# Splitting the first activation chunks and loading their weights further ahead, in a fused encoder block on one Trainium2 core

## The chip, the cores and the metric

One NeuronCore of a Trainium2 chip runs the whole program in one launch. Its engines work side by side, each in its own program order: PE (TensorE, matrix products), DVE (VectorE), ACT (ScalarE), POOL (GpSimd) and SP (SyncE, which here only issues DMAs). Semaphores make an instruction wait for data from another engine or from a DMA. The metric is the device time of one execution in microseconds; a change is judged by the median of several executions.

## The reference, cut to what matters

The block has 512 tokens of width 1024. First comes an adaLN-conditioned mixer (a gated convolution and a gated recurrence, one input and one output projection), then a PEER layer: every token looks up its best 16 of 16384 one-neuron experts in each of 8 heads and adds their outputs. The change lies in the PEER layer:

```python
def block(xb):                                   # in the reference over blocks of 128 tokens
    q = (xb @ w_q).reshape(p, PEER_HEADS, 2, PEER_DK_HALF)
    sc = jnp.einsum('phcd,hcnd->phcn', q, sub_keys)
    top_s, top_i = lax.top_k(sc, PEER_TOPK)      # 16 best of 128 keys, twice a head
    cand_s = (top_s[:, :, 0, :, None] + top_s[:, :, 1, None, :]).reshape(p, PEER_HEADS, kk)
    best_s, best_pos = lax.top_k(cand_s, PEER_TOPK)
    idx = jnp.take_along_axis(cand_i, best_pos, axis=-1)
    g = jax.nn.softmax(best_s, axis=-1)
    act = jax.nn.gelu(jnp.einsum('phkd,pd->phk', expert_u[idx], xb), approximate=False)
    return jnp.einsum('phk,phkd->pd', g * act, expert_v[idx])
```

## The kernel before

The kernel does the PEER layer in two ways at once. For 320 of the 512 tokens it is **dense**: all 16384 activations of a token are computed, multiplied by a gate matrix that is zero except at the token's 128 chosen experts, and multiplied by all of expert_v. For the other 192 tokens it is **sparse**: the chosen rows of expert_u and expert_v are gathered from HBM by POOL's indirect DMAs (L1044), and DVE makes dot products (L1065, in `dots`) and sums (L1082, in `sums`) of them. 64 of the sparse tokens (index tile `idx_b`) take only their dot products this way.

The dense half has 128 chunks of 128 experts. The first phase (L1277 to L1325, the loop over k below CE = 124) is the activation phase: step k makes the products of expert_u chunk k with the 320 tokens on PE (`u_chunk`), eight blocks of 128 in depth, and ACT applies Gelu into a tile (`u_evict`, L1149). The second phase (L1364 to L1394) multiplies the gated activations by the chunks of expert_v (`v_chunk`, L1348). Four expert_u chunks are left for the second phase.

Precision: a float32 operand is split into a high part in the faster fp32r format and a low part that holds the rest. `high` (L74) is an ACT copy, `low` (L79) a subtraction on DVE or on POOL; `mm3` (L88 to L90) makes three products a block: high by high, high by low, low by high. Chunks 1 to 11 (k below FN = 12) are different: they use the unsplit float32 weights and an unsplit copy of the tokens, `h2f`, with one matmul a block (L1158), and need neither high nor low. ACT writes `h2f` at L674, in the norm before the query projection.

Weights are loaded by SP, 512 KB a chunk, into a rotating pool `wraw` of WR = 4 tiles; chunks 5 to 11 use the pools `wlo` and `whi` in place of it. `w_ahead(k)`, called at the start of step k, issues loads up to chunk k + 4. High halves are made three steps ahead (`w_high(k + 3)`), low halves two steps ahead (`w_low(k + 2)`).

Activations of two chunks share a tile `act` of 2 x 320 columns, 16 of them (RB = 32 chunks). The first 48 pairs are written to HBM at step 2q + 4 (`spill`, to `Ad`) and read back in the second phase (`v_act`); the last ones stay in SBUF. Pairs 48 and up (v0 = 96) come first in the second phase.

The order of the activation phase is written out by a planner in the Python code (L1244 to L1315). It keeps counters of nanoseconds for PE, DVE and ACT (`pe`, `dve`, `ac`). Each step adds the costs of its chunk (L1166 to L1168) and then gives DVE pieces of other work until `dve` has caught up with `pe`: searches for the best keys (`topk_tile`, `stage1`), the gate matrix (`gates_tile`, with products of one-hot matrices on PE, L908) and dot products. A generator that yields a number has done work of that cost; one that yields None sleeps until the next step. What is not done by step KD = 118 is done there at once. The limit on dot products a step stands in `turn` (L1254): given["d"] counts them against DR = 1.25 a step, and `xd > k % 2` allows one in even steps and two in odd ones. The first gathers start when the search of token tile 1 has yielded its indices (`sready`).

The instructions from L670 to L1275 are ordered by the tile framework, which may move an instruction ahead of others on its engine; those of the loop stay in the order written.

Of the kernel before, what the change touches and what calls it, by code (L numbers as in the profile page):

```python
# [17 lines left out]
T = 512  # L18
# [16 lines left out]
def block_kernel(ctx, tc, xT, small, w_ada1, w_ada, b_ada, w_in, w_r, w_i, w_out, w_q, keys, uT, u, v, final_g, out):  # L35
# [618 lines left out]
    h2f = [ring.tile([128, 2, NU], F32, name="act", bufs=RB // 2) for _ in range(KB // 2)]  # L654
# [12 lines left out]
    for k in range(KB):  # L667
        if k == 2:
            qsp[1] = split_w(qraw[1])
            norm2.close()  # L670
        t1 = sq_pool.tile([128, T], F32, name="mt1")
        nc.vector.tensor_mul(t1, xs[:, k, :], psr2)
        modulate(t1, k, A2, adac[:, 24:32], h2h, h2l, full2)
        nc.scalar.activation(h2f[k // 2][:, k % 2], t1[:, T - NU:], AF.Identity, scale=A2[:, k:k + 1],  # L674
                             bias=adac[:, 24 + k:25 + k])
        if k < len(x1p):
            x1_out(*x1p[k])
# [61 lines left out]
    act0 = ring.tile([128, 2, NU], F32, name="act", bufs=RB // 2)  # L739
# [39 lines left out]
    def topk_tile(t):  # L779
# [30 lines left out]
        for w in range(2):  # L810
# [5 lines left out]
            if t == 1 and w == 0:  # L816
                yield None
# [281 lines left out]
    def w_load(k):  # L1099
        if k < len(jobs):  # L1100
            kind, i = jobs[k]
            if 5 <= k < FN:
                raw = wring.tile([128, KB, 128], FR, name=("wlo", "whi")[k % 2], bufs=WB).bitcast(F32)
                nc.sync.dma_start(raw, uT[i])
                wraw[k] = raw
                return
            if k >= K5 and (k - K5) % 5 == 4:
                wraw[k] = gp.tile([128, KB, 128], F32, name="raw5")
                nc.sync.dma_start(wraw[k], uT[i] if kind == "u" else
                                  v[vorder[i] * 128:(vorder[i] + 1) * 128, :].rearrange("p (k e) -> p k e", k=KB))  # L1110
                return
            wraw[k] = load_w(uT[i] if kind == "u" else
                             v[vorder[i] * 128:(vorder[i] + 1) * 128, :].rearrange("p (k e) -> p k e", k=KB))

    def w_high(k):
        if FN <= k < len(jobs):
            whi[k] = high(wraw[k])

    def w_low(k):
        if FN <= k < len(jobs):  # L1120
            wlo[k] = low(wraw.pop(k), whi[k])
            settle()
# [3 lines left out]
    def w_ahead(k):  # L1126
        while loaded[0] < k + (5 if k < K5 - 5 else 6):
            loaded[0] += 1
            w_load(loaded[0])
# [14 lines left out]
    def u_evict():  # L1144
        if unread:
            c, ps = unread.pop()
            if c % 2 == 0:
                act[c // 2] = ring.tile([128, 2, NU], F32, name="act", bufs=RB // 2)
            nc.scalar.activation(act[c // 2][:, c % 2], ps, AF.Gelu)  # L1149

    def u_chunk(k, pool):
        c = jobs[k][1]
        if c:
            ps = pool.tile([128, NU], F32, name="ps_act", bufs=3 if pool is psE else 2)
            if k < FN:
                raw = wraw.pop(k)
                for j in range(KB):
                    nc.tensor.matmul(ps, raw[:, j, :], h2f[j // 2][:, j % 2], start=j == 0, stop=j == KB - 1)  # L1158
            else:
                mm3(ps, whi.pop(k), wlo.pop(k), hd, ld, range(KB), True, True)  # L1160
# [5 lines left out]
        pe[0] += FPE if c and k < FN else 3530  # L1166
        dve[0] += 0 if c and k < FN - 2 else 1140
        ac[0] += 450 if c and k < FN - 3 else 1400  # L1168
# [41 lines left out]
    def v_act(q):  # L1210
        if q < NE // 2:
            c = vorder[2 * q] // 2
            if act[c] is None:
                act[c] = ring.tile([128, 2, NU], F32, name="act", bufs=RB // 2)
# [29 lines left out]
    pe, dve, ac = [0], [-HEAD], [0]  # L1244
# [6 lines left out]
    def turn(k):  # L1251

        awake = [g for g in "gsrd" if g in gens and asleep[g] <= k]
        if "d" in awake and (given["d"] >= DR * (k + 1 - first[0]) + DX * max(k - late_k.get("g", k), 0) or k >= CE - QU or xd > k % 2):  # L1254
            awake.remove("d")
# [21 lines left out]
    for k in range(CE):  # L1277
# [13 lines left out]
        dve[0] = max(dve[0], RHO * pe[0] - LEAD - (HEAD if k < 9 else 0))  # L1291
# [157 lines left out]
FN = 12  # L1449
DX = 0.3  # L1450
FPE = 4400
# [6 lines left out]
HEAD = 0  # L1458
# [9 lines left out]
RB = 32  # L1468
ZL = 1
# [54 lines left out]
```

## Time and profile before

| | us |
|---|---|
| median of 3 runs | 1323.59 |
| lowest and highest run | 1322.09, 1323.73 |
| the profiled execution | 1322.02 |
| its span | 1320.3 |
| PE, DVE, ACT, POOL busy in the span | 1302.8, 1210.0, 729.6, 508.7 |
| HBM read and written | 393.54 MB, 45.09 MB |

The span runs from the first to the last instruction; 1.7 us of the profiled execution lie around it. In time order: the mixer until about 207 us, norm and query projection until 279, the activation phase until about 773, the second phase until 1307, the last norm and the output until 1320. The page's line of DMA traffic, in 40 slices of 33 us:

```profile
GB/s 374 268 245 175 183 137 96 113 153 107 297 367 337 317 346 386 402 389 348 417 417 417 412 343 397 412 414 415 413 414 413 414 413 415 411 409 412 413 380 142
```

Slices 9 and 10 (280 to 330 us), the start of the activation phase, move little; from slice 19 on the rate is near 415 most of the time. Matmuls are pipelined, and the profile shows each with more time than passes between two of them, so the time of a chunk is read from the starts of successive chunks.

### The profile page before, as it was taken

Reading aid. Unit: us, or ns where it says so; the run is one execution under the profiler, and the core shown is the slowest. Engines: PE = TensorE matmul, PEld = TensorE weight load, DVE = VectorE, ACT = ScalarE, POOL = GpSimd, SP = SyncE. Lnnn points to the kernel's source line nnn. Section 1 sums busy time; section 2 is a strip of 40 time slices with the busy share of each in tenths; the row PEclk is TensorE's granted clock in tenths of the full one; section 3 lists DMA queues with packets and bytes.
Section 4 is the critical chain, followed back from the end, with each engine's and each line's share of the span. In section 5 each row is a group of like instructions: output and inputs, shape, how many; then the busy total and the mean of one; then the engine's idle time right before and its main releaser. Section 6 shows DMA issues by size and latency. Waiting matters only on the chain.

```text
span 1320.3 us, 21362 instructions
## 1 busy us (share of the span) xinstructions
PE 1302.8 (99%) x7506; PEld 1127.5 (85%) x7506; DVE 1210.0 (92%) x2241; ACT 729.6 (55%) x1319; POOL 508.7 (39%) x342
## 2 busy tenths in 40 slices
PE   8999999999999999999999999999999999999996
PEld 6677777777999999999999998888888888888885
DVE  6889975899999999999999679999899999899998
ACT  4677736424786987879669544333343434343433
POOL 0000002301133133434665537677555455565550
PEclk9999999999999999999999999999999999999999
DMA  9775542343899899999999999999999999999993
GB/s 374 268 245 175 183 137 96 113 153 107 297 367 337 317 346 386 402 389 348 417 417 417 412 343 397 412 414 415 413 414 413 414 413 415 411 409 412 413 380 142
DMA packets 151276, 440.06 MB, mean 333 GB/s; under 512 B 17024, under 2 KB 44672, under 8 KB 151168
## 3 DMA queue, kind: packets, MB, share of 16 engines
q1 hardware_dynamic: 104016, 267.23, 54.1%
q0 software_dynamic: 46864, 170.41, 32.7%
q8 instruction: 59, 0.97, 0.3%
q10 hardware_dynamic: 288, 1.05, 0.2%
q14 instruction: 49, 0.40, 0.1%
HBM read 393.54 MB, written 45.09 MB: 332 GB/s over the span
## 4 chain that ended last, share of the span: by engine, by line
PE 87%; issue 4%; DVE 3%; DMA 2%; POOL 2%; ACT 1%; DVEq 0%; SPq 0%; POOLq 0%; ACTq 0%
PE acc L1348 38%; PE ps_act L88 8%; PE ps_act L89 8%; PE ps_act L90 8%; PE ps_z L89 4%; PE ps_z L90 4%; PE ps_z L88 4%; PE ps_act L1158 4%; PE ps_gt L908 2%; POOL rows L1044 2%; PE ps_z L346 1%; DMA wraw<-in_uT_dram 1%; DMA rows<-in_u_dram,idx_s 1%; PE ps_g L732 1%; PE ps_row L138 1%
## 5 line engine op out<-in xcount | busy, mean ns | idle before, releaser
L74 ACT ACTIVATE whi<-wraw 128x1024 fp32r<-128x1024 f32 x255 | 269.7, 1058 | 235.6 <-DMA wraw<-in_v_dram 141.6
L79 DVE TENSOR_TENSOR wlo<-wraw,whi 128x1024 fp32r<-128x1024 f32 x249 | 303.2, 1218 | 34.4 <-ACT whi L74 33.7
L88 PE MATMUL ps_act<-h,whi 128*128 128x320 f32 x928 | 291.4, 314 | 0.0
L89 PE MATMUL ps_act<-h,whi 128*128 128x320 f32 x928 | 286.8, 309 | 0.0
L90 PE MATMUL ps_act<-h,wlo 128*128 128x320 f32 x928 | 286.7, 309 | 0.0
L1044 POOL DMA_INDIRECT rows<-in_u_dram,idx_s x128 | 207.5, 1621 | 142.5 <-DVE scr L1065 101.3
L1044 POOL DMA_INDIRECT rows<-in_v_dram,idx_s x128 | 192.1, 1501 | 158.3 <-DVE ys L1082 135.2
L1348 PE MATMUL acc<-wlo,ch 128*128 128x512 f32 x744 | 229.1, 389 | 0.0
L1348 PE MATMUL acc<-whi,ch 128*128 128x512 f32 x744 | 229.1, 389 | 0.0
L1348 PE MATMUL acc<-whi,cl 128*128 128x512 f32 x744 | 229.0, 389 | 0.0
L88 PEld LDWEIGHTS ps_act<-h,whi 128*128 128x128 f32 x928 | 174.2, 188 | 0.5
L89 PEld LDWEIGHTS ps_act<-h,whi 128*128 128x128 f32 x928 | 174.4, 188 | 0.2
L90 PEld LDWEIGHTS ps_act<-h,wlo 128*128 128x128 f32 x928 | 174.2, 188 | 0.0
L1044 POOL DMA_INDIRECT rows<-in_u_dram,idx_b x64 | 88.5, 1382 | 215.9 <-DVE scr L1065 152.9
L1082 DVE SCALAR_TENSOR_TENSOR ys<-rows,acts,ys 128x1024 f32<-128x1024 f32 x127 | 163.3, 1286 | 1.5
L1348 PEld LDWEIGHTS acc<-wlo,ch 128*128 128x128 f32 x744 | 139.7, 188 | 29.0
L1348 PEld LDWEIGHTS acc<-whi,cl 128*128 128x128 f32 x744 | 139.7, 188 | 29.0
L1348 PEld LDWEIGHTS acc<-whi,ch 128*128 128x128 f32 x744 | 139.5, 188 | 28.5
L1065 DVE SCALAR_TENSOR_TENSOR scr<-rows,h2n 128x1024 f16<-128x1024 f32 x128 | 156.1, 1220 | 6.7 <-DMA rows<-in_u_dram,idx_s 5.1
L1149 ACT ACTIVATE act<-ps_act 128x320 f32<-128x320 f32 x127 | 55.7, 439 | 112.7 <-PE ps_act L90 79.4
L896 ACT ACTIVATE igh<-oh,gl 128x128 f16<-128x128 f16 x320 | 99.5, 431 | 4.5 <-DVE oh L875 4.5
L1232 ACT ACTIVATE ch<-cf 128x768 fp32r<-128x768 f32 x64 | 54.2, 847 | 61.8 <-PE acc L1348 20.7
(326 smaller groups left out, 1884.1 us busy)
## 6 DMA issues: line engine op xcount, KB each, us to landing
wraw<-in_uT_dram SPq DMA_DIRECT2D x120, 512.0 KB, 7.6
wraw<-in_v_dram SPq DMA_DIRECT2D x103, 512.0 KB, 13.4
Gd<-stg SPq DMA_DIRECT2D x46, 512.0 KB, 9.1
wada<-in_w_ada_dram SPq DMA_DIRECT2D x45, 512.0 KB, 6.5
Ad<-act SPq DMA_DIRECT2D x48, 320.0 KB, 8.1
act<-Ad SPq DMA_DIRECT2D x48, 320.0 KB, 14.2
raw<-in_v_dram SPq DMA_DIRECT2D x25, 512.0 KB, 13.3
h<-Gd SPq DMA_DIRECT2D x48, 256.0 KB, 14.4
```

The lines of the kernel that those rows point to most:

```text
L74: nc.scalar.activation(hi, raw, AF.Copy)
L79: (eng or nc.vector).tensor_sub(lo, raw, hi.bitcast(F32))
L88: nc.tensor.matmul(ps, hi[:, k, :], xh(k), start=first and k == ks[0], stop=False)
L89: nc.tensor.matmul(ps, hi[:, k, :], xl(k), start=False, stop=False)
L90: nc.tensor.matmul(ps, lo[:, k, :], xh(k), start=False, stop=last and k == ks[-1])
L896: nc.scalar.activation(ig[:, 1, k // 2, :, k % 2], of[:, k // 2, 0, :, k % 2], AF.Copy, scale=gl[:, t0 + k:t0 + k + 1])
L1044: nc.gpsimd.indirect_dma_start(out=r[:, :], out_offset=None, in_=table, in_offset=bass.IndirectOffsetOnAxis(ap=idxs[:, k:k + 1], axis=0))
L1065: nc.vector.scalar_tensor_tensor(scr, rows.pop(n), 1.0, hn, op0=OP.mult, op1=OP.mult, accum_out=dst[:, k:k + 1])
L1082: nc.vector.scalar_tensor_tensor(ys, rows.pop(k), acts[:, k:k + 1], ys, op0=OP.mult, op1=OP.add)
L1149: nc.scalar.activation(act[c // 2][:, c % 2], ps, AF.Gelu)
L1232: nc.scalar.activation(ch, coef[q], AF.Copy)
L1348: nc.tensor.matmul(accs[b][e], st[:, bs], mv[:, e * 512:(e + 1) * 512], start=first, stop=last)
```

## The change

Chunks 1 to 11 go through `high`, `low` and `mm3` like the others; `h2f` and its eight ACT copies are gone. The low halves of chunks 1 to 9 (k below PL = 10) are made on POOL, the others on DVE. The 16 activation tiles become one tile `ringb`. Its first seven slots of 1024 columns (PB = 7) take weights as long as the activations kept there are not due (slot r until chunk v0 + 2 * (1024r // 640), that is 96, 98, 102, 104, 108, 112, 114); the spilled pairs use the last four activation slots in turn (SPS = 4). `w_ahead` issues up to two loads a step as slots come free, which gives up to 12 chunks ahead (7 slots and the 4 tiles of `wraw`), until k = 112. The planner's costs follow: 3530 for every chunk on PE, a low half on DVE is charged from step 8 on. The search of token tile 1 sleeps three more steps in all, and from step 92 on each step may take two dot products.

```diff
--- before.py
+++ after.py
@@ -651,7 +651,11 @@
     ring = ctx.enter_context(tc.tile_pool(name="ring", bufs=1, side="right"))
     ND = T - 128
     NU = ND - XB
-    h2f = [ring.tile([128, 2, NU], F32, name="act", bufs=RB // 2) for _ in range(KB // 2)]
+    ringb = ring.tile([128, RB * NU], F32, name="ringb")
+
+    def act_slot(i):
+        return ringb[:, 2 * NU * i:2 * NU * (i + 1)].rearrange("p (c t) -> p c t", c=2)
+
 
     def full2(k, f):
         if k % 4 == 0:
@@ -671,8 +675,6 @@
         t1 = sq_pool.tile([128, T], F32, name="mt1")
         nc.vector.tensor_mul(t1, xs[:, k, :], psr2)
         modulate(t1, k, A2, adac[:, 24:32], h2h, h2l, full2)
-        nc.scalar.activation(h2f[k // 2][:, k % 2], t1[:, T - NU:], AF.Identity, scale=A2[:, k:k + 1],
-                             bias=adac[:, 24 + k:25 + k])
         if k < len(x1p):
             x1_out(*x1p[k])
 
@@ -736,7 +738,7 @@
         for c in range(2):
             sc[h, c] = scs.tile([128, NT, 128], F32, name="sc", bufs=SCB)
             nc.scalar.activation(sc[h, c], pss[c], AF.Copy)
-    act0 = ring.tile([128, 2, NU], F32, name="act", bufs=RB // 2)
+    act0 = act_slot(RB // 2 - SPS)
     nc.scalar.activation(act0[:, 0], ps0, AF.Gelu)
     assert next(early, None) is None
     pro.close()
@@ -813,7 +815,8 @@
                 pf = topk.tile([128, 8, 16], F16, name="pf")
                 nc.vector.tensor_copy(pf, msk)
             yield None
-            if t == 1 and w == 0:
+            if t == 1:
+                yield None
                 yield None
             key, ref, cmp, src = ((pf, st16, OP.is_ge, dif), (pf, io16, OP.is_equal, tif[:, :, 1, :]))[w]
             nc.scalar.activation(oh, key[:, :, :, None].to_broadcast(shp), AF.Copy)
@@ -1096,37 +1099,51 @@
     v0 = max(CE - RB + 3, 0) // 8 * 8 + 8
     vorder = list(range(v0, NE)) + list(range(v0))
 
-    def w_load(k):
+    rfree, rold = [0] * PB, []
+
+    def w_load(k, at=0):
         if k < len(jobs):
             kind, i = jobs[k]
-            if 5 <= k < FN:
-                raw = wring.tile([128, KB, 128], FR, name=("wlo", "whi")[k % 2], bufs=WB).bitcast(F32)
-                nc.sync.dma_start(raw, uT[i])
-                wraw[k] = raw
-                return
             if k >= K5 and (k - K5) % 5 == 4:
                 wraw[k] = gp.tile([128, KB, 128], F32, name="raw5")
                 nc.sync.dma_start(wraw[k], uT[i] if kind == "u" else
                                   v[vorder[i] * 128:(vorder[i] + 1) * 128, :].rearrange("p (k e) -> p k e", k=KB))
                 return
+            for r in range(PB):
+                if 5 <= k <= v0 + 2 * (1024 * r // (2 * NU)) and rfree[r] <= at:
+                    rfree[r] = k - 1
+                    wraw[k] = ringb[:, 1024 * r:1024 * (r + 1)].rearrange("p (k e) -> p k e", k=KB)
+                    nc.sync.dma_start(wraw[k], uT[i])
+                    return
+            if k < K5 - 5:
+                assert len(rold) < WR or rold[-WR] <= at
+                rold.append(k - 1)
             wraw[k] = load_w(uT[i] if kind == "u" else
                              v[vorder[i] * 128:(vorder[i] + 1) * 128, :].rearrange("p (k e) -> p k e", k=KB))
 
     def w_high(k):
-        if FN <= k < len(jobs):
+        if k < len(jobs):
             whi[k] = high(wraw[k])
 
     def w_low(k):
-        if FN <= k < len(jobs):
-            wlo[k] = low(wraw.pop(k), whi[k])
+        if k < len(jobs):
+            wlo[k] = low(wraw.pop(k), whi[k], nc.gpsimd if k < PL else None)
             settle()
 
     loaded = [4]
 
     def w_ahead(k):
+        if k < K5 - 13:
+            for _ in range(2):
+                m = loaded[0] + 1
+                if any(f <= k and 5 <= m <= v0 + 2 * (1024 * r // (2 * NU)) for r, f in enumerate(rfree)) \
+                        or len(rold) < WR or rold[-WR] <= k:
+                    loaded[0] += 1
+                    w_load(m, k)
+            return
         while loaded[0] < k + (5 if k < K5 - 5 else 6):
             loaded[0] += 1
-            w_load(loaded[0])
+            w_load(loaded[0], k)
 
     def weights(k):
         w_ahead(k)
@@ -1145,27 +1162,23 @@
         if unread:
             c, ps = unread.pop()
             if c % 2 == 0:
-                act[c // 2] = ring.tile([128, 2, NU], F32, name="act", bufs=RB // 2)
+                q = c // 2
+                act[q] = act_slot(q - v0 // 2 if q >= v0 // 2 else RB // 2 - SPS + q % SPS)
             nc.scalar.activation(act[c // 2][:, c % 2], ps, AF.Gelu)
 
     def u_chunk(k, pool):
         c = jobs[k][1]
         if c:
             ps = pool.tile([128, NU], F32, name="ps_act", bufs=3 if pool is psE else 2)
-            if k < FN:
-                raw = wraw.pop(k)
-                for j in range(KB):
-                    nc.tensor.matmul(ps, raw[:, j, :], h2f[j // 2][:, j % 2], start=j == 0, stop=j == KB - 1)
-            else:
-                mm3(ps, whi.pop(k), wlo.pop(k), hd, ld, range(KB), True, True)
+            mm3(ps, whi.pop(k), wlo.pop(k), hd, ld, range(KB), True, True)
             u_evict()
             unread.append((c, ps))
         q = c // 2 - 2
         if c % 2 == 0 and 0 <= q < v0 // 2:
             spill(q)
-        pe[0] += FPE if c and k < FN else 3530
-        dve[0] += 0 if c and k < FN - 2 else 1140
-        ac[0] += 450 if c and k < FN - 3 else 1400
+        pe[0] += 3530
+        dve[0] += 0 if k < PL - 2 else 1140
+        ac[0] += 1400
 
     gbuf, g16, gdone = {}, {}, set()
     coef = {}
@@ -1211,7 +1224,7 @@
         if q < NE // 2:
             c = vorder[2 * q] // 2
             if act[c] is None:
-                act[c] = ring.tile([128, 2, NU], F32, name="act", bufs=RB // 2)
+                act[c] = act_slot(c % (RB // 2))
                 nc.sync.dma_start(act[c].rearrange("p c t -> p (c t)"), Ad[c])
 
     def v_gated(q):
@@ -1241,7 +1254,7 @@
 
     gens = {"s": searches_E(), "r": rest_E(), "g": gates_E(), "d": dots()}
     dot_gen = gens["d"]
-    pe, dve, ac = [0], [-HEAD], [0]
+    pe, dve, ac = [0], [0], [0]
     late_k = {}
     asleep = {"s": 0, "r": 0, "g": 0, "d": NE}
     given = {"s": 0, "r": 0, "g": 0, "d": 0}
@@ -1251,7 +1264,7 @@
     def turn(k):
 
         awake = [g for g in "gsrd" if g in gens and asleep[g] <= k]
-        if "d" in awake and (given["d"] >= DR * (k + 1 - first[0]) + DX * max(k - late_k.get("g", k), 0) or k >= CE - QU or xd > k % 2):
+        if "d" in awake and (given["d"] >= DR * (k + 1 - first[0]) + DX * max(k - late_k.get("g", k), 0) or k >= CE - QU or xd > (k % 2 if k < 92 else 1)):
             awake.remove("d")
         if gopen and "g" in gens:
             gt = 96 * (k + 1 - gopen[0]) / (KD - KG - gopen[0])
@@ -1288,7 +1301,7 @@
             for m in range(GB_E - 1):
                 gath(u, usteps[m][0], usteps[m][3], m)
         ac[0] = max(ac[0], pe[0] - LEAD)
-        dve[0] = max(dve[0], RHO * pe[0] - LEAD - (HEAD if k < 9 else 0))
+        dve[0] = max(dve[0], RHO * pe[0] - LEAD)
         xd = 0
         while dve[0] < RHO * pe[0] or k == KD:
             g = turn(k)
@@ -1446,16 +1459,14 @@
 GS = 32768.0
 AB = 3
 GPE = 460
-FN = 12
+PL = 10
 DX = 0.3
-FPE = 4400
 SE = 0.65
 AD = 500
 LEAD = 3500
 RHO = 1.0
 VE = 1
 KG = 4
-HEAD = 0
 NS = 56000
 DS = 1.0
 XD = 2
@@ -1466,6 +1477,8 @@
 QU = 6
 UV = 0.86
 RB = 32
+PB = 7
+SPS = 4
 ZL = 1
 XE = 5
 WB = 4
```

## The prediction

> **What bounds the kernel now.** I read the page first, for the engines' shares, then the table of stretches, to see whether one engine is the limit everywhere, then the timelines of TensorE (PE) and VectorE (DVE) chunk by chunk.
>
> ```profile
> span 1320.3 us, 21362 instructions
> ## 1 busy us (share of the span) xinstructions
> PE 1302.8 (99%) x7506; PEld 1127.5 (85%) x7506; DVE 1210.0 (92%) x2241; ACT 729.6 (55%) x1319; POOL 508.7 (39%) x342
> ```
>
> ```profile
> 212.90:228.80 15.90, 14.99 (x80) 9.49 (x78) 15.23 (x25) 15.49 (x24) 2.25 (x4) 1.00 0.37 129
> 280.00:327.00 47.00, 47.00 (x177) 33.23 (x176) 45.99 (x270) 14.18 (x20) 2.91 (x3) 1.00 0.35 119
> 327.00:420.00 93.00, 93.00 (x703) 92.27 (x702) 92.31 (x227) 66.13 (x140) 33.55 (x23) 1.00 0.94 326
> 420.00:526.00 106.00, 106.00 (x866) 104.16 (x866) 105.09 (x243) 92.68 (x212) 25.61 (x20) 1.00 0.96 352
> 640.00:735.00 95.00, 95.00 (x742) 93.68 (x741) 86.81 (x124) 74.31 (x195) 56.87 (x37) 1.00 1.03 417
> 735.00:770.00 35.00, 35.00 (x240) 35.00 (x240) 20.51 (x25) 14.07 (x22) 12.40 (x8) 1.00 1.04 390
> ```
>
> The columns are the stretch, its length, then PE, weight loads, DVE, ScalarE (ACT), GpSimd (POOL), the granted clock, the DMA share and GB/s. PE is busy in the whole activation phase (about 279 to 773 us), at full clock. DVE is close behind it up to 526 us (45.99 of 47, 92.31 of 93, 105.09 of 106) and has room only after 640 us. DMA runs at 417 GB/s from 640 to 735 us. So time is saved where PE has less to do or stops standing, as long as DVE keeps up. The same chain in the last phase:
>
> ```profile
> 803.16 489.62 PE acc L1348 x2160
> ```
>
> That is 227 ns for each of 2160 matmuls without a break, and the change adds nothing there: what the activation phase saves should reach the end.
>
> **The change, part by part. 1. Eleven chunks in three matmuls for one.**
>
> ```profile
> 296.57 4.47 PE L1158 MATMUL ps_act<-act,whi 128*128 128x320 f32 x16
> 300.88 4.47 PE L1158 MATMUL ps_act<-act,wlo 128*128 128x320 f32 x16
> ...
> 334.08 0.31 PE L88 MATMUL ps_act<-h,whi 128*128 128x320 f32 x1
> ...
> 337.60 0.31 PE L88 MATMUL ps_act<-h,whi 128*128 128x320 f32 x1
> ```
>
> One unsplit chunk takes 300.88 - 296.57 = 4.31 us, a split one (334.08 to 337.60, chunk 14) 3.52. Eleven chunks: 11 x 0.79 = **8.7 us less on PE**. [...]
>
> **2. The stand of PE at 632 us.**
>
> ```profile
> 631.18 1.06 ACT L74 ACTIVATE whi<-wraw 128x1024 fp32r<-128x1024 f32 x1 [2.97 <-DMA wraw<-in_uT_dram]
> ...
> 632.62 2.27 PE L908 MATMUL ps_gt<-igh,oh 128*128 128x128 f16 x15 [0.30 <-ACT igh L896]
> ...
> 641.98 0.93 PE ps_gt L908 x16
> ```
>
> ACT stood 2.97 us for a weight load, the gate products behind it on ACT (L896) came late, and PE, after 0.30 us idle, spent 2.27 us on 15 gate matmuls, 2.6 in all, where 16 usually take 0.93. It is the only place where chunk starts show such a stand. Loads issued up to 12 chunks ahead (they were 4) take that wait away: **1.7 us less**. Nothing else is late next there: DVE idles 8.2 us of that stretch.
>
> **3. Eight ACT copies into h2f go (L674).**
>
> ```profile
> L674 ACT ACTIVATE act<-mt,adac,A 128x320 f32<-128x320 f32 x8 | 5.1, 643 | 0.0
> ```
>
> 5.1 us of ACT, in a stretch (212.9 to 228.8) where ACT is busy 15.49 of 15.90 us. But DVE is busy 15.23 there, so no more than 0.7 can be had; bounds 0 and 0.7, I take **0.4 less**.
>
> **4. DVE's lead at the start.** The planner (L1244 to 1315) gives DVE work until its counter passes PE's. Walking through its counters for both versions gives the work of each step. Before, step 0 charged a low half (1140) that nobody made, and PE's first chunks were charged 4400 but took 4.31; both made a lead. After, lows 1 to 9 are charged nothing and chunks 3530 against a real 3.52.
>
> ```profile
> 281.36 0.27 DVE L690 MAX8 top<-sc 128x8 f32<-128x128 f32 x1
> ...
> 293.50 0.29 DVE L690 MAX8 top<-sc 128x8 f32<-128x128 f32 x1
> ...
> 322.62 1.22 DVE L79 TENSOR_TENSOR wlo<-wraw,whi 128x1024 fp32r<-128x1024 f32 x1
> 323.76 0.28 DVE L832 SCALAR_TENSOR_TENSOR best<-ij 128x128 f32<-128x128 f32 x1
> ...
> 335.46 1.20 DVE L79 TENSOR_TENSOR wlo<-wraw,whi 128x1024 fp32r<-128x1024 f32 x1
> ```
>
> The lead is thin already: chunk 15's low half ends at 336.66, and the chunk starts at 337.60. After: steps 0 to 2 have the same work as before, 281.36 to 293.50. Steps 3 to 6 have 11 half searches, 13.05 by the planner's costs, which the trace bears out for this kind; step 7 has 4.2 to 4.4. So the first low half on DVE (chunk 10) starts near 311.0 and ends near 312.1. PE would ask for it at 279.24 + 9 x 3.52 + 0.3 = 311.2. Seven low halves (1.14 each, 322.62 to 323.76) and 17.6 us of work later, chunk 17's ends near 337.8; PE would ask for it at 335.9. Past that the gate matmuls give PE more to do. So PE stands about **2.0 us** in all between chunks 10 and 17 (it is the largest lateness, not the sum). Bounds: 0, if DVE runs quicker than its planned costs, and 3.
>
> **5. Nine low halves on GpSimd, high halves on ACT.**
>
> ```profile
> L79 POOL TENSOR_TENSOR wlo<-wraw,whi 128x1024 fp32r<-128x1024 f32 x6 | 14.2, 2377 | 23.1 <-ACT whi L74 23.1
> ...
> 280.32 1.02 POOL L767 DMA_INDIRECT rows<-in_u_dram,ssum  x1 [0.75 <-POOL ssum L766]
> ...
> 279.24 17.49 PE L1158 MATMUL ps_act<-act,wraw 128*128 128x320 f32 x64
> ...
> L74 ACT ACTIVATE whi<-wraw 128x1024 fp32r<-128x1024 f32 x255 | 269.7, 1058 | 235.6 <-DMA wraw<-in_v_dram 141.6
> ```
>
> A low half takes 2.38 us on POOL, shorter than a chunk. Low 1 lies outside the hand-ordered part and can be made while PE still works on w_q, as were the six before. Low 2 stands behind POOL's first gather (ends 281.34), so it ends near 283.8 while PE asks at 283.1: 0.7 us, inside the 2.0 of part 4. ACT's 11 high halves (1.06 each, 11.6 us) fit, as ACT is busy 14.18 of 47 us. Without that cover each late one would cost its own 1.06.
>
> But POOL and DVE get in each other's way in this trace:
>
> ```profile
> 283.71 0.87 DVE L784 TENSOR_TENSOR oh<-top 128x128 f32<-128x128 f32 x4
> ...
> 291.80 0.27 DVE L798 TENSOR_TENSOR g<-best 128x128 f32<-128x128 f32 x1
> ...
> 326.00 0.94 POOL L1044 DMA_INDIRECT rows<-in_u_dram,idx_b  x1 [0.31 <-issue]
> ...
> 386.29 1.98 POOL L1044 DMA_INDIRECT rows<-in_u_dram,idx_b  x1 [0.30 <-issue]
> ...
> 386.24 1.22 DVE L1065 SCALAR_TENSOR_TENSOR scr<-rows,h2b 128x1024 f16<-128x1024 f32 x1
> ```
>
> The same gather takes 0.94 us beside one-operand searches and 1.98 beside two-operand DVE work. No row shows a low half on POOL beside two-operand DVE work (the six ran beside searches). After the change POOL makes lows without pause from about 281.4 to 298, and DVE has two bursts of short two-operand operations there: L784 to L791 at 283.7 and L798 to L804 at 291.8. Bounds: 0, and a wait of one low for nearly every operation of the first burst, 6 x 2.38 = 14.3 us. I take one wait for each burst, of half to a whole low (1.2 to 2.4 each): **3.0 us**, added to DVE's lateness. It is nearer to the lower end because a burst's next operation follows within 0.2 us.
>
> **6. What moves at no cost.** The planner's counters end with 118 dot products made by the end of the phase (117 before), gates finished at step 116 (113) and the first gathers four steps later (the extra yields); all fits ahead of step 118. On SP a load now waits for low k+1 instead of k at step k; behind it stand spills and gate stores. Only four activation slots serve the spilled blocks, so the Gelu of block 2q+8 waits for spill q, with high halves and gate products behind it on ACT and PE behind those. That leaves about 4 chunks, 14 us, for a spill that lands in 8.1 us at the median (row below). Cover gone: each us late is one for PE, after three PSUM buffers.
>
> **Sum.** 1322.0 (the profiled execution) - 8.7 - 1.7 - 0.4 + 2.0 + 3.0 = 1316.2. That execution lies 1.6 below the median of the runs shown, 1323.6; the same difference from the median gives 1317.8. I forecast **1317**.
>
> **Rivals.** *No trouble between POOL and DVE* (20%): the 3.0 goes: 1313.2 to 1314.8. For it: searches take one operand and six lows ran at 2.38 undisturbed.
>
> *DVE and POOL take turns* (12%, the slower side): every operation of L784 to L791 waits for a whole low. 14.3 in place of 3.0: 1327.5 to 1329. It cancels the gain from 8.8 us of such waits on. For it: 0.94 against 1.98. Against it: the bursts are short. [...]
>
> *Dot products starve late* (13%).
>
> ```profile
> rows<-in_u_dram,idx_s POOLq DMA_INDIRECT x128, 8.9
> ...
> Ad<-act SPq DMA_DIRECT2D x48, 320.0 KB, 8.1
> ```
>
> ```profile
> 744.98 1.22 DVE L1065 SCALAR_TENSOR_TENSOR scr<-rows,h2n 128x1024 f16<-128x1024 f32 x1 [1.26 <-DMA rows<-in_u_dram,idx_s]
> ```
>
> From step 92 on every chunk may take two dots (before: one and two in turn). Five row buffers with 8.9 us landing, 0.6 start and 1.2 use allow one dot in 10.7 / 5 = 2.1 us; two a chunk want 1.76. 26 such dots lose 26 x 0.38 = 9.9 us against a DVE lead of about 8; at 11 us landing they lose 19. PE would stand 2 to 6 us: 1319 to 1323.
>
> *The first low half comes late* (7%): low 1 lands behind POOL's gather, and PE stands 4.5 us at 279 instead of 2.0: 1319 to 1321.
>
> **How the numbers follow.** Forecast as summed 48%, the rivals 20, 12, 13 and 7. The range from 1311 (no POOL trouble, 1 us of DVE lateness) to 1324 leaves out the turns and little else. About 0.2% (2.6 us) is what a measurement of this kernel can tell from no change: faster 0.80, same 0.11 (late dots, half of the milder turns), slower 0.09.
>
> **What would show it.** PE's chunks 1 to 11 start 3.52 us apart, except for a stand that DVE's low half ends near chunk 10 to 17; DVE's L784 or L798 with idle time ahead, ended by POOL; no wait of ACT for uT loads at 87 to 95; the last phase again 227 ns a matmul. I am wrong if PE stands at new places after chunk 90, or if the last phase grows.

## The result, and the profile after

The changed kernel takes 1336.39 us (median of six runs, 1332.95 to 1342.34) against 1322.84 for the kernel before beside it: ratio 1.0106, 95% interval 1.0095 to 1.0118. It is about 1% slower. The forecast was 1317. The profiled execution of the changed kernel took 1332.95, with a span of 1330.9, so its trace shows 10.6 us of the loss.

The page of the kernel after:

```profile
span 1330.9 us, 21581 instructions
PE 1297.3 (97%) x7594; PEld 1134.7 (85%) x7594; DVE 1220.3 (92%) x2243; ACT 734.2 (55%) x1322; POOL 528.3 (40%) x351
```

Its table of stretches (stretch, length, PE, weight loads, DVE, ACT, POOL, granted clock, DMA share, GB/s), then the first stretch in the kernel before:

```profile
210.00:225.00 15.00, 11.41 (x60) 7.78 (x59) 9.41 (x20) 9.20 (x14) 4.07 (x9) 0.77 0.86 324
280.00:327.00 47.00, 40.95 (x274) 40.38 (x273) 46.22 (x256) 21.12 (x29) 17.81 (x9) 0.93 0.43 136
327.00:420.00 93.00, 92.55 (x698) 91.76 (x697) 92.00 (x245) 67.53 (x138) 28.34 (x21) 1.00 0.88 309
420.00:526.00 106.00, 106.00 (x856) 104.56 (x855) 104.35 (x265) 87.49 (x198) 22.68 (x15) 1.00 0.94 333
735.00:770.00 35.00, 29.78 (x209) 28.89 (x208) 25.50 (x35) 17.17 (x38) 17.85 (x13) 1.00 0.99 362
```

```profile
210.00:225.00 15.00, 14.10 (x87) 9.60 (x86) 12.87 (x26) 13.65 (x23) 4.13 (x8) 1.00 0.46 176
```

PE now stands in three places: in the second norm (11.41 of 15.00 us busy, at a clock of 0.77; before 14.10, at 1.00), near chunk 10 (40.95 of 47.00; before 47.00), and at the phase's end (29.78 of 35.00; before 35.00). DVE is still close to full from 280 to 526 us (46.22 of 47, 92.00 of 93, 104.35 of 106) and has about as much to do as before; from 327 us on PE is full as well.

**The first place** is the second norm. SP's and ACT's timelines of the kernel after, then ACT's of the kernel before (start, duration, operation, and in brackets the idle time ahead of it with what ended it):

```profile
197.27 0.33 SPq L1116 DMA_DIRECT2D ringb<-in_uT_dram  x1
...
198.78 8.23 SPq L1116 DMA_DIRECT2D ringb<-in_uT_dram  x6
...
216.09 0.60 ACT L594 ACTIVATE xn<-ps_z 128x512 f32<-128x512 f32 x1 [4.64 <-DMA x1d<-xn]
```

```profile
212.05 0.60 ACT L594 ACTIVATE xn<-ps_z 128x512 f32<-128x512 f32 x1 [0.55 <-DMA x1d<-xn]
```

The seven slot loads of w_load wait for nothing once the ring is a plain tile, so the scheduler issued them at 197 to 206 us. Beside them the eight stores into x1d landed late (5.5 us at the median instead of 2.4), ACT stood 4.64 us for a free xn buffer instead of 0.55, PE stood too and then had a granted clock of 0.50 from 216.6 to 223.2 us, and its first activation chunk started at 283.27 instead of 279.24: **4.0 us**.

**The second** is chunk 10. PE's timeline after, from its wait for the low half to the end of the slow matmuls, then DVE's and POOL's:

```profile
321.55 0.64 PE L90 MATMUL ps_act<-h,wlo 128*128 128x320 f32 x1 [6.05 <-DVE wlo L79]
321.98 0.47 PE L88 MATMUL ps_act<-h,whi 128*128 128x320 f32 x1
322.25 0.47 PE L89 MATMUL ps_act<-h,whi 128*128 128x320 f32 x1
...
325.45 0.45 PE L89 MATMUL ps_act<-h,whi 128*128 128x320 f32 x1
...
325.88 0.30 PE L88 MATMUL ps_act<-h,whi 128*128 128x320 f32 x1
326.02 0.31 PE L89 MATMUL ps_act<-h,whi 128*128 128x320 f32 x1
```

```profile
283.67 2.13 DVE L756 TENSOR_SCALAR rep<-iota 128x16 f32<-128x16 f32 x1
...
289.51 2.20 DVE L786 TENSOR_TENSOR oh<-top 128x128 f32<-128x128 f32 x4
...
299.39 2.38 DVE L803 SCALAR_TENSOR_TENSOR msk<-pos,msk 128x128 uint32<-128x128 uint32 x1
```

```profile
283.32 2.41 POOL L79 TENSOR_TENSOR wlo<-wraw,whi 128x1024 fp32r<-128x1024 f32 x1 [1.18 <-ACT whi L74]
...
288.55 2.40 POOL L79 TENSOR_TENSOR wlo<-ringb,whi 128x1024 fp32r<-128x1024 f32 x1 [1.49 <-ACT whi L74]
...
299.11 2.50 POOL L79 TENSOR_TENSOR wlo<-ringb,whi 128x1024 fp32r<-128x1024 f32 x1 [1.10 <-ACT whi L74]
```

Chunks 1 to 9 take 31.78 us (283.27 to 315.05), 3.53 each, as forecast. Then PE waits 6.05 us for the first low half that DVE makes. Three DVE operations started inside a low half on POOL, and each ends within 0.2 us of the end of that low half: L756 after 2.13 us instead of 0.16, the first of L786's four (the four together take 2.20 instead of 0.87), and L803 after 2.38 instead of 0.29. DVE shows no idle time there; the wait lies inside the duration. After the stand PE's matmuls start 0.267 us apart instead of 0.147 for 4.2 us. Chunk 10 took 11.7 us instead of 3.5: **8.2**, which nearly uses up part 1's gain.

**The third** is the end of the phase. DVE's timeline of the kernel after, then the view of waits (us in total, times, longest) of the kernel after and of the kernel before:

```profile
751.42 1.23 DVE L1068 SCALAR_TENSOR_TENSOR scr<-rows,h2n 128x1024 f16<-128x1024 f32 x1 [4.06 <-DMA rows<-in_u_dram,idx_s]
754.86 1.23 DVE L1068 SCALAR_TENSOR_TENSOR scr<-rows,h2n 128x1024 f16<-128x1024 f32 x1 [2.21 <-DMA rows<-in_u_dram,idx_s]
...
778.78 0.83 DVE L1238 TENSOR_TENSOR cf<-ringb,gt 128x640 f32<-128x640 f32 x1 [3.22 <-DMA gt<-Gd]
```

```profile
DVE scr L1068 <- DMA rows<-in_u_dram,idx_s: 14.8, 14, 4.1
```

```profile
DVE scr L1065 <- DMA rows<-in_u_dram,idx_s: 5.1, 6, 2.0
```

DVE waits for gathered rows, low halves queue behind the dots, and PE stands in chunks 118 to 120: 6.0 us. In chunk 123 it stands 1.6 more, and there DVE waits for a read of the gate matrix (3.22 us for gt from Gd), not for a row. Together **7.6 us**. The last phase is as before:

```profile
813.72 489.62 PE acc L1361 x2160
```

So 4.0 + 8.2 + 7.6 = 19.8 us are lost, and 8.4 in chunks 1 to 11 and 1.7 near 632 us are gained; smaller stands in between make up the rest of 10.6.

### The profile page after: what moved, and what is told of

It is laid out like the page before. It is cut to its first block, busy times and chain, and to the rows that moved or that the text cites. A ratio compares the mean times of both kernels' runs of the same rounds, so it can differ in the third digit from the quotient of the medians.

```text
span 1330.9 us, 21581 instructions
## 1 busy us (share of the span) xinstructions
PE 1297.3 (97%) x7594; PEld 1134.7 (85%) x7594; DVE 1220.3 (92%) x2243; ACT 734.2 (55%) x1322; POOL 528.3 (40%) x351
## 4 chain that ended last, share of the span: by engine, by line
PE 74%; DVE 12%; DMA 8%; issue 3%; POOL 2%; ACT 1%; DVEq 0%; SPq 0%; POOLq 0%; ACTq 0%
PE acc L1361 38%; PE ps_act L88 6%; PE ps_act L90 6%; PE ps_act L89 6%; DMA rows<-in_u_dram,idx_s 5%; PE ps_z L88 3%; PE ps_z L89 3%; PE ps_z L90 3%; PE ps_gt L911 2%; POOL rows L1047 2%; DVE rep L696 1%; DVE wlo L79 1%; PE ps_z L346 1%; DVE ti L701 1%; DVE ti L694 1%
## 5 line engine op out<-in xcount | busy, mean ns | idle before, releaser
L74 ACT ACTIVATE whi<-wraw 128x1024 fp32r<-128x1024 f32 x197 | 208.1, 1058 | 242.8 <-DMA wraw<-in_v_dram 134.9
L90 PE MATMUL ps_act<-h,wlo 128*128 128x320 f32 x1016 | 315.6, 311 | 11.3 <-DVE wlo L79 11.3
L88 PE MATMUL ps_act<-h,whi 128*128 128x320 f32 x1016 | 319.7, 315 | 0.0
L89 PE MATMUL ps_act<-h,whi 128*128 128x320 f32 x1016 | 315.2, 310 | 0.0
L79 DVE TENSOR_TENSOR wlo<-wraw,whi 128x1024 fp32r<-128x1024 f32 x187 | 229.3, 1228 | 26.2 <-ACT whi L74 25.5
L1047 POOL DMA_INDIRECT rows<-in_u_dram,idx_s x128 | 196.9, 1539 | 123.2 <-DVE scr L1068 92.3
L90 PEld LDWEIGHTS ps_act<-h,wlo 128*128 128x128 f32 x1016 | 191.6, 189 | 12.3 <-DVE wlo L79 12.3
L88 PEld LDWEIGHTS ps_act<-h,whi 128*128 128x128 f32 x1016 | 191.6, 189 | 0.4
L89 PEld LDWEIGHTS ps_act<-h,whi 128*128 128x128 f32 x1016 | 191.7, 189 | 0.2
L1047 POOL DMA_INDIRECT rows<-in_u_dram,idx_b x64 | 98.0, 1532 | 218.6 <-DVE scr L1068 164.6
L1167 ACT ACTIVATE ringb<-ps_act 128x320 f32<-128x320 f32 x127 | 55.6, 438 | 101.1 <-PE ps_act L90 100.9
```

What stands on the lines that cost most here:

```text
L74: nc.scalar.activation(hi, raw, AF.Copy)
L79: (eng or nc.vector).tensor_sub(lo, raw, hi.bitcast(F32))
L88: nc.tensor.matmul(ps, hi[:, k, :], xh(k), start=first and k == ks[0], stop=False)
L89: nc.tensor.matmul(ps, hi[:, k, :], xl(k), start=False, stop=False)
L90: nc.tensor.matmul(ps, lo[:, k, :], xh(k), start=False, stop=last and k == ks[-1])
L1047: nc.gpsimd.indirect_dma_start(out=r[:, :], out_offset=None, in_=table, in_offset=bass.IndirectOffsetOnAxis(ap=idxs[:, k:k + 1], axis=0))
```

## The experiments

Each was timed beside the kernel before; ratios are to it.

| run | edit | median us | ratio (95%) |
|---|---|---|---|
| after | | 1336.4 | 1.0106 (1.0095–1.0118) |
| e1_hold | slot loads held back | 1330.9 | 1.0055 (1.0039–1.0072) |
| e2_xd | old limit of dots | 1335.5 | 1.0089 (1.0072–1.0105) |
| e3_nolow | no low halves on GpSimd | 1332.4 | 1.0053 (1.0035–1.0071) |
| e4_sleep | old yields | 1338.9 | 1.0125 (1.0101–1.0150) |
| e5_lead | e1 + DVE lead | 1329.5 | 1.0056 (1.0042–1.0070) |
| e13_base | e1 + old limit | 1330.9 | 1.0065 (1.0051–1.0079) |
| e6_less | e13, 8 dots left out | 1320.5 | 0.9985 (0.9976–0.9994) |
| e7_lead_less | e6 + DVE lead | 1318.5 | 0.9969 (0.9959–0.9980) |
| e8_before_less | before, 8 dots left out | 1321.8 | 0.9994 (0.9984–1.0003) |
| e11_dve | e13, 8 gathers left out | 1322.8 | 1.0004 (0.9995–1.0013) |
| e12_dma | e13, 8 dots out, gathers kept | 1329.0 | 1.0044 (1.0031–1.0058) |
| e9_pool18 | 17 low halves on GpSimd | 1325.9 | 1.0021 (1.0012–1.0030) |
| e10_pool14 | 13 low halves on GpSimd | 1332.2 | 1.0072 (1.0057–1.0086) |

### e1_hold: are the hoisted loads the first loss?

```diff
             x1_out(*x1p[k])
+    nc.vector.tensor_copy(ringb[:, 0:PB * 1024].rearrange("p (r n) -> p r n", n=1024)[:, :, 0], h2n[:, 512:512 + PB])
```

> The changed kernel, with one tiny DVE copy (7 elements a partition, from h2n) into the seven load slots behind the second norm, so that their loads can start only after it. Theory A (the seven slot loads, issued at 197 to 205 us, held up the x1d stores and so ACT, DVE and PE in the second norm): the slot loads are issued after 228 us, the x1d stores land within 3 us again, PE's first activation chunk starts near 279.3 instead of 283.3, and the time falls by about 4 us, to about 1332. Rival B (the eight copies taken out of the norm let the scheduler order it worse, or the granted clock fell for another reason): the first chunk still starts at 283, and the time stays within 1 us of 1336.4.

SP's and ACT's timelines of e1_hold, and its stretch of the second norm:

```profile
231.78 0.33 SPq L1117 DMA_DIRECT2D ringb<-in_uT_dram  x1
...
212.34 0.60 ACT L594 ACTIVATE xn<-ps_z 128x512 f32<-128x512 f32 x1 [0.55 <-DMA x1d<-xn]
```

```profile
210.00:225.00 15.00, 14.12 (x87) 10.05 (x86) 12.92 (x22) 11.60 (x18) 7.06 (x9) 1.00 0.48 176
```

Theory A holds: ACT waits 0.55 us again, PE works 14.12 us of 15, chunk 1 starts at 279.31. The median falls by 5.5. All of the 4.0 us are there up to chunk 10, but only 2.2 of the span: by chunk 113 half is given back, in stands that are longer than in the kernel after, by 0.7 at chunk 10, 0.5 at 102 and 1.2 at 107.

### e2_xd: are two dots a step the late loss?

```diff
-        if "d" in awake and (... or xd > (k % 2 if k < 92 else 1)):
+        if "d" in awake and (... or xd > k % 2):
```

> The changed kernel with the old limit of dot products in a step (one and two in turn up to the end). 110 instead of 118 dots are then planned for the activation phase, the other 8 go into the last phase, where DVE has room. Theory A (two gathered rows a step cannot be landed from step 92 on, so DVE and then PE stand from chunk 113 on): PE's stands from chunk 118 to 123 shrink from 7.6 to under 2 us, the longest wait of DVE for a row falls from 4.06 to under 2.2 us, and the time falls by 6 to 8, to about 1329. Rival B (the gate stores, three steps later than before, hold up the end): the stands stay, and the time is within 2 us of 1336.4. Rival C (the 8 dots come back in the last phase): the stands go, but the time falls by less than 4.

The stands of chunks 118 to 120 go, yet the time falls by only 0.9, inside the intervals: Rival C. The phase's end comes 4.4 us earlier (chunk 123 at 773.6 instead of 778.0), but with 8 dots more to make, the last phase ends later than the one of the kernel after: from its first to its last matmul it takes 548.2 us instead of 537.1. What starved late was a symptom; here 8 dots have no cheap place in either phase. The stand at chunk 123 goes too, so whether the late gate read there followed from the crowd of dots or stood by itself is not settled.

### e3_nolow and e4_sleep

```diff
-            wlo[k] = low(wraw.pop(k), whi[k], nc.gpsimd if k < PL else None)
+            wlo[k] = whi[k] if k < PL else low(wraw.pop(k), whi[k])
```

> The changed kernel with chunks 1 to 9 multiplying the high half a second time where the low half stood, so that GpSimd makes no low halves (the low part of these nine chunks is left out of the result). PE, ACT and DVE have the same instructions as in the changed kernel. Theory A (GpSimd's low halves lengthen DVE's operations beside them by 5.2 us in all before chunk 10): L756, L786 and L803 take 0.2 to 0.3 us again instead of 2.1, 1.6 and 2.4, PE stands 1 to 2 us near chunk 10 to 17 instead of 6.05, no matmuls at a lower clock follow it, and the time falls by 6 to 7, to about 1330. Rival B (the planner's lead is too small by itself): DVE's operations are as short, but the low half of chunk 10 is still over 4 us late, and the time falls by less than 2.

DVE's and PE's timelines in e3_nolow:

```profile
286.05 0.16 DVE L756 TENSOR_SCALAR rep<-iota 128x16 f32<-128x16 f32 x1
...
290.52 0.89 DVE L786 TENSOR_TENSOR oh<-top 128x128 f32<-128x128 f32 x4
...
299.08 0.29 DVE L803 SCALAR_TENSOR_TENSOR msk<-pos,msk 128x128 uint32<-128x128 uint32 x1
...
319.25 0.41 PE L90 MATMUL ps_act<-h,wlo 128*128 128x320 f32 x1 [1.39 <-DVE wlo L79]
```

Theory A's mechanism holds: without low halves on POOL the three operations are short, PE waits 1.39 instead of 6.05 us, and no slow matmuls follow. Its size is not settled: the five executions scatter from 1328.0 to 1333.1, the median falls by 4.0, and the ratio to the kernel before by 0.0053, which would be 7. In the trace the first chunk started 2.4 later (the granted clock was 0.89 from 10 to 25 us, 1.00 in the kernel after), and 6.5 us saved at chunk 10 shrank through stands at chunks 17, 21, 101 and 123.

```diff
-            if t == 1:
-                yield None
+            if t == 1 and w == 0:
                 yield None
```

> The changed kernel with the old, shorter yields in the second tile's search (one in place of four). The first gathers are then issued at step 16 instead of 19; the dots planned for the phase stay at 119 (118). Theory A (what starves DVE late is two dots a step from step 92 on): the stands from chunk 118 on stay between 5 and 9 us, and the time is within 2 us of 1336.4. Rival B (the dots began too late, and this is caught up at the end): the stands fall under 3 us, and the time falls by 5 or more.

Rival B falls: gathers that begin three steps earlier make the time no shorter, and by its median 2.5 longer. Theory A isn't confirmed by it either: the stands from chunk 118 on are 5.5 us (3.9 and 1.6 at 118 and 119), inside its 5 to 9, but 5.6 more came at chunks 107 and 108, the longest wait for a row fell to 1.8, and the time is 2.5 off, not within 2.

### e5_lead: does a stand that is taken away stay away?

```diff
-    pe, dve, ac = [0], [0], [0]
+    pe, dve, ac = [0], [3000], [0]
```

> The kernel of e1_hold with the planner's DVE counter started at 3000 instead of 0, so that by its own costs DVE gets 25.3 instead of 29.5 us of work in steps 0 to 7, and chunk 10's low half comes 4.2 us earlier; 117 dots in the phase (118). Theory A (the stand at chunk 10 is a loss of its own, and what is saved there stays saved): chunk 10, 8.9 us too long in e1_hold, is at most 2.5 too long, and the time falls by 6 to 8, to 1323 to 1325. Theory D (from chunk 90 on the phase is paced by rows, which DMA and DVE deliver no faster, so that PE meets later what it saves earlier): chunk 10 as in A, but the stands from chunk 90 to 123 grow by over 3 us, and the time falls by less than 3.5, to 1327.5 or more.

Chunk 10 is 1.9 too long instead of 8.9, as planned, yet the time falls by 1.4 only, which is Theory D's size and not A's. D's reason is not borne out: chunks 90 to 123 take 144.7 us here and 144.8 in e1_hold, so the stands there did not grow. The saving was given back earlier, in pieces of 0.5 to 1.6 us at chunks 12, 17, 18, 22, 42 and 53. In the trace chunk 1 also began 1.5 later (280.80 for 279.31; the granted clock was 0.89 from 10 to 25 us, 1.00 in e1_hold); counted from chunk 1 on, this run is 3.2 shorter. By the ratios nothing is gained (1.0056 and 1.0055). So at most about half of the 7.0 us is kept.

### e6_less, e7_lead_less, e8_before_less: what 8 dots cost

```diff
-    usteps = [...] + [(idx_s, h2n, acts, k) for k in range(128)]
+    usteps = [...] + [(idx_s, h2n, acts, k) for k in range(120)]
...
             if n == XB + 70:
+                nc.vector.tensor_copy(acts[:, 120:128], h2n[:, 0:8])
```

> The kernel of e1_hold with the old limit of dots in a step, and with the last 8 of the 192 dot products left out (their 8 coefficients are other numbers). Per dot this is 0.5 MB of gather and 1.25 us of DVE. Theory D (the changed phase is shorter, so 8 dots fewer fit into it, and the last phase has no DMA time for them): without these 8 the stands from 118 on go as in e2_xd, the last phase again takes 489.6 us for 2160 matmuls, and the time falls to 1323 to 1326, 5 to 8 below e1_hold. Rival (the last phase of e2_xd was slower for another reason): it stays slower, and the time is 1329 or more.

> The three edits together: slot loads held back, DVE's counter started at 3000, the old limit of dots with 8 dots left out. If the losses found so far are all (4 in the second norm, 8 at chunk 10, 5 to 7 late, that is 17 to 19 of 1336.4), the time is 1316 to 1320, near the forecast of 1317. If the saving at chunk 10 is given back later whatever the number of dots, it is no more than 2 below e6_less.

> The kernel before with the same 8 dots left out, for control. Theory D: PE has no stand there that a dot makes, so the time is within 2 us of 1323. Rival (fewer dots are a gain in any kernel of this kind): it falls by 5 or more, and e6_less and e7_lead_less show nothing about the change.

Stretches of e7_lead_less, then the last link of its chain of waits:

```profile
280.00:327.00 47.00, 44.97 (x305) 44.44 (x304) 46.30 (x243) 25.34 (x33) 15.36 (x8) 1.00 0.52 169
327.00:420.00 93.00, 92.03 (x691) 90.71 (x690) 92.23 (x237) 64.94 (x135) 31.51 (x21) 1.00 0.89 315
420.00:526.00 106.00, 104.03 (x840) 102.27 (x839) 103.62 (x266) 88.07 (x202) 19.57 (x14) 1.00 0.91 318
```

```profile
799.55 489.62 PE acc L1363 x2160
```

e6_less is 10.4 below e1_hold, more than was expected; the same 8 dots cost the kernel before 0.6, which its interval doesn't tell from nothing. In the traces the difference sits in chunks 90 to 123: they take 133.9 us before, 143.1 after, 144.8 in e1_hold and 134.8 in e6_less. With the lead as well e7_lead_less takes 1318.5. That is near the forecast, but with 8 dots less work than the forecast was for; against the kernel before with the same dots left out it is 3.3 less. The lead adds 2.0 where it took 7 off chunk 10: DVE is close to full in all three stretches (46.30 of 47, 92.23 of 93, 103.62 of 106), and PE, once ahead, waits in small pieces, for DVE in most of them and for ACT in the largest (1.6 us in chunk 42).

### e13_base, e11_dve, e12_dma: gather or arithmetic?

```diff
 (e11_dve)
-            nc.vector.scalar_tensor_tensor(scr, rows.pop(n), 1.0, hn, ...)
+            nc.vector.scalar_tensor_tensor(scr, rows.pop(n) if n < XB + 120 else hn, 1.0, hn, ...)
...
-                gath(u, usteps[m][0], usteps[m][3], m)
+                if m < XB + 120:
+                    gath(u, usteps[m][0], usteps[m][3], m)
 (e12_dma)
+            if n < XB + 120:
                 nc.vector.scalar_tensor_tensor(scr, rows.pop(n), 1.0, hn, ...)
+            else:
+                rows.pop(n)
```

> The kernel of e1_hold with the old limit of dots and all 192 dots: the step between e1_hold and e6_less, and the base for the two runs that split the price of the 8 late dots. From e2_xd (1335.5) less what e1_hold saved (4.0 to 5.5): 1330 to 1331.5. If the old limit gains something once the slot loads are held back: 1328 or less.

> The same with the last 8 dot products made from h2n instead of a gathered row (8 coefficients are other numbers), so that DVE has all 192, and DMA and GpSimd 8 gathers less (4.2 MB). Theory M (the last phase has no DMA time for 8 more gathers): within 2 of e6_less's 1320.5. Theory V (DVE has no time for 8 more dots, 10 us): within 3 of e13_base. If both limits hold, it stands between.

> The opposite: the last 8 rows are gathered, but their dot products are left out (8 coefficients are other numbers). Theory M: within 3 of e13_base. Theory V: within 2 of e6_less's 1320.5.

Stretches of the last phase, first of e13_base, then of e11_dve, and last two of the longest links in e13_base's chain of waits:

```profile
900.00:1000.00 100.00, 99.07 (x435) 81.03 (x434) 93.79 (x115) 38.17 (x49) 64.20 (x40) 1.00 1.03 414
1100.00:1200.00 100.00, 98.78 (x434) 80.90 (x433) 95.18 (x89) 39.15 (x51) 61.97 (x38) 1.00 1.03 414
1280.00:1300.00 20.00, 17.06 (x75) 13.55 (x73) 19.89 (x19) 9.41 (x12) 8.03 (x5) 1.00 0.96 366
1310.00:1320.00 10.00, 7.02 (x31) 5.46 (x30) 9.46 (x21) 3.93 (x12) 0.00 (x0) 1.00 0.27 105
```

```profile
900.00:1000.00 100.00, 99.34 (x439) 81.94 (x438) 95.90 (x118) 41.05 (x53) 52.37 (x33) 1.00 1.01 393
1280.00:1300.00 20.00, 19.31 (x86) 15.66 (x85) 19.89 (x21) 7.47 (x11) 4.83 (x3) 1.00 0.74 289
1310.00:1320.00 10.00, 0.00 (x0) 0.00 (x0) 6.06 (x16) 1.77 (x7) 0.00 (x0) 0.57 0.41 157
```

```profile
1201.61 16.03 DMA h<-Gd
...
1229.56 14.17 DMA wraw<-in_v_dram
```

Mostly theory M: dropping the gathers and keeping DVE's work takes 8.1 us off, dropping DVE's work and keeping the gathers 1.9. e11_dve stays 2.3 above e6_less, just outside M's mark of 2, so DVE's work has a small part. e11_dve takes 8 gathers off GpSimd too, but GpSimd is not full there (64.20 of 100 us in e13_base). Eight gathers are 8 x 0.524 = 4.2 MB, and at the 414 GB/s that the last phase moves up to 1200 us, 10.1 us. In the kernel before the chain of waits is PE alone here (489.62 us); in e13_base it runs over DMA, here reads of the gate matrix (Gd) and of expert_v, and from its first to its last matmul the last phase takes 546.5 us, against 536.8 both before and in e6_less. In e13_base DMA still moves 366 GB/s at 1280 to 1300 us, where e11_dve is down to 289, and PE works on past 1310, where e11_dve's has ended. e13_base also shows where the loss sits in the end: its first matmul of the last phase starts at 770.56, 2.0 us ahead of the kernel before (772.52), and the kernel ends 8.8 behind it by the medians.

### e9_pool18 and e10_pool14: a faster version?

```diff
-PL = 10
+PL = 18
-    pe, dve, ac = [0], [0], [0]
+    pe, dve, ac = [0], [1500], [0]
```

together with the edits of e1_hold, e2_xd and e4_sleep; e10_pool14 has PL = 14.

> An attempt at a version faster than both. The kernel of e1_hold with the old limit of dots, the old shorter yields, the planner's DVE counter started at 1500, and 17 instead of 9 low halves on GpSimd (PL 18). Planned: first gathers at step 15, 115 dots in the phase (117 before, 111 for the same kernel with PL 10). Theory D (DVE is what the phase lacks: eight low halves fewer are 9.1 us of DVE, spent on dots early, when DMA has room): no low half on DVE before chunk 18, so no stand at chunk 10, no stands from 118 on, and a time of 1317 to 1323. Rival (GpSimd's low halves lengthen DVE's two-operand operations by as much as they save DVE): DVE comes late at chunk 18 by 4 or more, and the time is 1326 or more.

> The same with 13 low halves on GpSimd (PL 14), all of them ahead of the first gather of the dot products on GpSimd; 112 dots planned. Theory D: between e1_hold and e9_pool18, 1321 to 1327. Rival (lengthened DVE operations): no faster than e1_hold's 1330.9. If it is faster than e9_pool18, the four low halves behind the first gathers on GpSimd came late and held PE there.

DVE's, POOL's and ACT's timelines of e9_pool18:

```profile
308.49 3.31 DVE L828 TENSOR_TENSOR oh<-oh,dif 128x2048 f16<-128x2048 f16 x1
...
304.97 9.10 POOL L79 TENSOR_TENSOR wlo<-ringb,whi 128x1024 fp32r<-128x1024 f32 x3 [7.54 <-ACT whi L74]
...
316.09 1.91 ACT L822 ACTIVATE oh<-pf 128x2048 f16<-128x2048 f16 x1 [8.65 <-DVE pf L817]
```

e9_pool18 is 10 us faster than the change, but 0.2% slower than the kernel before, and between the two expectations: no stand is left from chunk 90 on, but chunks 10 to 18 lose 12.6 us. L828 takes 3.31 us beside a low half (1.23 in the kernel after, without one), and three of POOL's low halves take 9.10 together, 3.0 each instead of 2.4. But the longest stand of PE there, 3.6 us up to chunk 11, ends with ACT's Gelu, which stood behind L822: ACT waited 8.65 us there for DVE's search. This run has the shorter yields, so L822 comes closer behind the search than in the change; how much of the 12.6 is due to that and how much to POOL, no run tells apart. e10_pool14 has stands of the same size there (13.0), ends the phase 1.8 later, and is 6 slower. No version tried with all 192 dots beats the kernel before.

## Why the prediction was wrong, by its own steps

- **"What the activation phase saves should reach the end"** (the first part) failed. I quoted DVE at 45.99 of 47, 92.31 of 93 and 105.09 of 106, and still took PE for what is to be relieved. The planner hands DVE its work by PE's time. A phase that is 8.7 us shorter on PE, with two more low halves on DVE, leaves DVE room for fewer dots: they either crowd its end or go, with their gathers, into the last phase, where DMA is full (414 GB/s at a share of 1.03, 900 to 1000 us of e13_base).
- **Part 6, the dots** ("118 ... (117 before) ... all fits") counted dots and not when they come: by the planner's counters 71 instead of 78 by step 92. With the new limit of two a step they starve; under the old limit 110 are made, and the last phase grows. Price: 10.4 us (e1_hold less e6_less) against the 0 of the sum; of the price in the last phase 8.1 goes with the gathers (e11_dve). This is the largest missed term.
- **Part 6, the loads.** I looked at SP's waits at their place in the text of the program, not at how early the scheduler may issue a load that waits for nothing. Price: 4.0 us up to chunk 10 and 2.2 at the end in the traces, 5.5 in the medians (e1_hold), against 0.
- **Parts 1 and 2 were right.** Chunks at 3.53 us; chunk 87, with the stand at 632, takes 4.52 us instead of 6.22. The 8.2 us of idle DVE that part 2 names belong to 640 to 735 us, though; around the stand, from 625 to 640, DVE is busy 14.93 of 15.00. **Part 3** (0.4) can't be seen: with the loads held back chunk 1 starts at 279.31 and 279.04 in two kernels, before at 279.24.
- **Parts 4 and 5 were right in kind.** Together 5.0 us of DVE lateness was forecast and 6.05 came: 1.39 from the lead (e3_nolow; 0.9 forecast for chunk 10) and 4.7 from POOL (3.0 forecast, one wait in each of two bursts, which came as said; the third, on L756, I had not seen). The sign that was to show the waits was wrong: no idle time stands ahead of the DVE operations, their durations are longer. Two sizes were missing. After the 6.05 us stand the matmuls were slow (0.267 us apart instead of 0.147 for 4.2 us), which added about 2. And on the other side lateness in a stretch where DVE is nearly full cost less than its length here: taking 7 us of it away brought 1.4 and 2.0 by the medians (e5_lead, e7_lead_less), 3.2 and 2.5 in the traces counted from chunk 1.
- **The rivals.** "Dot products starve late" had 13% and happened (7.6 us instead of 2 to 6), but curing it alone bought nothing (e2_xd, e13_base). Three losses came together, while chances were given as if one excluded the others; no case added them up, and the range ended at 1324.

By the medians the way from 1336.4 to the 1318.5 of e7_lead_less is 5.5 (loads), 10.4 (dots) and 2.0 (lead). These are steps between successive kernels, so that they add up proves nothing by itself, and e6_less and e7_lead_less both have 8 dots left out. No run shows that the forecast of 1317 can be had with all the work. Open: why the stands of e1_hold at chunks 10, 102 and 107 are longer, so that half of its 4.0 us is lost by chunk 113, and whether the stands of e4_sleep have the same cause as those after the change.

## What to carry to other kernels

When two engines and the DMA are all nearly full, as here (PE 97% and DVE 92% of the span, DMA at 414 GB/s in the last phase), a saving on one is worth only what the others can follow: ask what the shorter phase pushes out of itself, and whether the place where it lands has room for its bytes. Here unsplit matmuls spent 0.79 us of PE a chunk to spare DVE, or GpSimd beside it, a low half (1.14 us on DVE); in a stretch where DVE is nearly full, no run here with all the dots gained by giving that up. And a load that waits for nothing may be issued far ahead of its place in the program, here at 197 us instead of after 231: tie it to something if it must not meet other transfers.

## What the runs showed of the hardware

The granted clock fell behind the 6.05 us stand. Windows of the kernel after:

```profile
315.00:321.60 6.60, 0.55 (x5) 0.29 (x3) 6.43 (x16) 1.40 (x2) 0.00 (x0) 0.80 0.00 1
321.60:325.70 4.10, 4.10 (x15) 4.10 (x16) 4.10 (x23) 0.00 (x0) 0.00 (x0) 0.50 0.41 128
325.70:327.00 1.30, 1.30 (x10) 1.30 (x10) 1.30 (x11) 0.04 (x1) 0.00 (x0) 0.98 0.74 88
```

It stood at 0.50 for 4.1 us of work. In e3_nolow, where PE waited 1.39 us at chunk 10, the matmuls behind the wait start 0.147 us apart, not 0.267. The length of a stand alone did not decide it, though: in e3_nolow PE also stood 1.75 us up to 781.0, and the granted clock was 0.79 from 782 to 790 us, while after e1_hold's stand of 1.80 us in the same chunk it was 1.00 there.

DVE's operations were held beside POOL's: L803, two operands, took 2.38 us beside a low half of 2.50, and 0.29 in e3_nolow, without low halves on POOL. No run had shown DVE held when the prediction was made; the rows quoted there show POOL held, a gather at 1.98 us instead of 0.94. L756, a TENSOR_SCALAR with one operand, was held too (2.13 us beside a low half of 2.41, 0.16 in e3_nolow).
